# Recurrence keys transposed on VectorE instead of TensorE in a Hymba block

## The chip, the cores and the metric

The kernel runs on one core of a Trainium2 chip. The metric is the device time of one execution in microseconds (us); the median of three runs is compared. A profiled execution of the same program gives the trace from which the rows below are taken. Engines are named as in the profile: PE is TensorE's matmul, PEld its weight load, DVE VectorE, ACT ScalarE, POOL GpSimd, SP the engine whose queue issues the DMAs. L12 is line 12 of the kernel's file.

## The reference, cut to what matters

One layer: 512 tokens behind 16 learned meta tokens, width 2048. The input is normalised and projected by one matrix of 8320 columns. About half of these columns feed an RWKV-7 recurrence of 16 heads of 64 channels, the other half a short gated convolution. Both halves are gated, concatenated, projected back, added to the residual and normalised.

```python
def step(S, inp):
    r_t, w_t, k_t, v_t, kk_t, b_t = inp
    sa = jnp.einsum('bhvk,bhk->bhv', S, kk_t)
    S = (S * w_t[:, :, None, :]
         - sa[..., None] * b_t[:, :, None, :]
         + v_t[..., None] * k_t[:, :, None, :])
    y_t = jnp.einsum('bhvk,bhk->bhv', S, r_t)
    return S, y_t
...
hn = _rmsnorm(h_res, norm_in_g[l])
P = hn @ w_in[l]
...
y = _rwkv7_recurrence(rh, decay, kh, vh, kk, kk * ah)
...
mix = jnp.concatenate([y_a, y_b], axis=-1)
h_res = h_res + mix @ w_out[l]
```

The state S of a head is updated with two kinds of keys: b (taken off) and k (put on). These two kinds are what the change is about.

## The kernel before

**Projection.** The input is kept feature-major in SBUF (128 features on the partitions, 528 tokens along them), split into a high part `xh` and a low part `xl`. Each of the 65 tiles of 128 projection columns is made by `main()`, which runs `steps()` (L315): for each of 16 k-tiles and two ranges of tokens three matmuls, wh times xh, wh times xl and wl times xh. The tiles are called by what they hold: k, r, v and g for a pair of heads, C, h, B and gc for a group of the convolution, lora once. Their order is the list `plan`.

**Weights.** `prefetch()` loads 1024 columns (L134, tile `wr`, three buffers), which are two quarters of a projection tile. `split_w()` makes of each quarter (512 columns) the high part `wh`, a cast on ACT (L126), and the low part `wl`, a subtraction on DVE for even quarters and on POOL for odd ones (L127). There are six buffers each of wh and wl. Quarters are numbered in the order in which they are used, four to a projection tile.

**Order.** PE's order is written by hand. `mains()` is a generator of projection matmuls; `fill(ns)` and `until()` draw from it between the other matmuls, so that the projection covers what the recurrence's preparation waits for. The order on DVE, ACT, POOL and SP is made by a scheduler from the program and its priorities. `later(ns, fn)` puts DMAs to a due time on the clock of the drawn projection matmuls.

**Pairs.** Heads are handled in eight pairs, two times 64 channels on 128 partitions, time in nine chunks of 64 (the first holds the 16 meta tokens). `prepare(i)` makes for pair i the decay (`tz`, L521 and L522, plus one on POOL L581, a running sum `cc` on DVE L583), the operands `ar` (kk with decay, r with decay; L607) and `bk` (the keys: b, k and b again, so that either head finds its two kinds side by side: for head 0 b then k, for head 1 k then b), and the gram matmuls (L625) of chunk by chunk bk against ar, masked on DVE (L635) into `gt`. PE then transposes (L655) the two kinds of keys of chunks 0 to 7 from feature-major to token-major, 64 partitions by 128 columns to 128 partitions by 64, for each chunk and head; two PSUM tiles `zz` hold the result, and ACT copies them (L661) to `bt`. Norms (`n2`) and the bonus (`zb`, copied to r) follow. Between them, `gt` is sent through DRAM into 16x16 blocks, `d` and `nd`, and inverted on DVE (L701 to L734, the inverse chain). `invert()` widens the inverses of two pairs to 64x64.

**Operands in DRAM.** For each pair there is a buffer `opd`, 9 chunks of 128 rows of 576 floats. `stash()` (L567) stores into it: `spot(i, row, rows_n, c0, cn, step, o, n)` is n floats at offset o of rows_n rows from row on, over cn chunks. The offsets of a row are fixed; b is at O_B = 448 and k at O_K = 512, 64 floats each.

**Recurrence.** `recur()` walks over the chunks, loads the operands of each pair (tile `ct`, two buffers each, L870), and makes of the state `st`, the inverses and the values the products `rz` (L889), `z` (L906), the state's update `zs` (L941) and the outputs `zy` (L945). In `zs` the keys are the weights: 64 tokens on the partitions by 64 features, one matmul with u for b and one with v for k, for each head. Chunk 8 needs no update of the state.

**Output.** `split_mix()` brings the gated results back, and the output projection (L1070) runs over them at the end.

Of the kernel before, what the change touches and what calls it, by code (L numbers as in the profile page):

```python
# [9 lines left out]
F32 = mybir.dt.float32  # L10
# [8 lines left out]
P = 128  # L19
# [5 lines left out]
CH = 64  # L25
NCH = SEQ // CH + 1
# [12 lines left out]
O_AR, O_KK, O_BR, O_X, O_V, O_B, O_K = 0, 128, 256, 320, 384, 448, 512  # L39
# [37 lines left out]
def hymba_kernel(ctx: ExitStack, tc: tile.TileContext, xt, xtok, w_in, w_out, pv, lup, cst, msk, gf, out):  # L77
    nc = tc.nc
# [10 lines left out]
    ident = cs[:, C_ID : C_ID + P]  # L89
# [52 lines left out]
    cq = ph2.enter_context(tc.tile_pool(name="cq", bufs=1, side="right", reuse_waits="tile"))  # L142
# [12 lines left out]
    pz = ph1.enter_context(tc.tile_pool(name="pz", bufs=2, space=PSUM))  # L155
# [355 lines left out]
    def until(*key):  # L511
        while key not in ready:
            step()
# [41 lines left out]
    heads = [(h, slice(64 * h, 64 * h + 64), slice(64 - 64 * h, 128 - 64 * h)) for h in range(2)]  # L555
# [4 lines left out]
    def spot(i, row, rows_n, c0, cn, step, o, n):  # L560
        d = opd[i]
        return bass.AP(
            tensor=d.tensor, offset=d.offset + (c0 * P + row) * OPW + o, ap=[[OPW, rows_n], [step * P * OPW, cn], [1, n]]
        )

    def stash(i, src, o, n, row=0, rows_n=P, c0=0, cn=NCH, step=1):
        nc.sync.dma_start(spot(i, row, rows_n, c0, cn, step, o, n), src)  # L567

    def prepare(i):
        p = i % 2  # L570
        until("k", i)
        k = got["k", i]
        ar = cq.tile([P, NCH, 2, CH], F32, tag="ar", name=f"ar{i}")
        bk = cq.tile([P, NCH, 3, CH], F32, tag="bk", name=f"bk{i}")
# [4 lines left out]
        tz = low_rank(i, 0, up, hv[:, 0, i : i + 1], f"tz{i}", -1.0)  # L579
# [38 lines left out]
        fill(FW["gram_b" if p else "gram"])  # L618

        gt = cq.tile([P, 2, NCH, P], F32, tag=f"gt{p}", name=f"gt{i}")  # L620
        bt = cq.tile([P, 2, NCH - 1, CH], F32, tag="bt", name=f"bt{i}")

        def gram(z, c, c0):
            for h, hs, ho in heads:
                nc.tensor.matmul(  # L625
                    z[h][:, c - c0],
                    bk[hs, c, h : h + 2, :].rearrange("p a s -> p (a s)"),
                    ar[hs, c].rearrange("p a s -> p (a s)"),
                    start=True, stop=True,
                )  # L630

        def masked(z, c0, c1):
            with ahead():
                for h in range(2):
                    nc.vector.tensor_tensor(  # L635
                        out=gt[:, h, c0:c1],
                        in0=z[h],
                        in1=gmask[:, h].unsqueeze(1).to_broadcast([P, c1 - c0, P]),
                        op=ALU.mult,
                    )  # L640
# [7 lines left out]
        masked(zc, 4, 8)  # L648
        fill(FW["gram2"])
        ze = [pi.tile([P, 1, P], F32, tag=("misc", "ser")[h], name=f"g{i}_8_{h}") for h in range(2)]  # L650
        zz = [pz.tile([P, NCH - 1, CH], F32, tag="tz", name=f"bt{i}_{h}") for h in range(2)]
        gram(ze, 8, 8)
        for c in range(NCH - 1):
            for h, hs, ho in heads:
                nc.tensor.transpose(  # L655
                    zz[h][:, c], bk[hs, c, h : h + 2, :].rearrange("p a s -> p (a s)"),
                    ident[hs, 64 * h : 64 * h + 64],
                )
        masked(ze, 8, 9)
        for h in range(2):  # L660
            nc.scalar.copy(bt[:, h], zz[h])  # L661
        fill(FW["gram3"])
        n2 = tr(f"n2{i}")
        for j, (a, b) in enumerate(((0, 288), (288, LP))):
# [26 lines left out]
        d = cq.tile([NB, 256], F32, tag="d", name=f"d{i}").rearrange("p (s t) -> p s t", t=16)  # L691
# [22 lines left out]
        for m in (2, 4, 8):  # L714
            for b in range(16 // (2 * m)):
                o = b * 2 * m
# [33 lines left out]
        later(16500 if p else 33000, load_inverse)  # L750

        for h, hs, ho in heads:
            stash(i, bt[hs, h], O_B, CH, 64 * h, 64, 0, NCH - 1)
            stash(i, bt[ho, h], O_K, CH, 64 * h, 64, 0, NCH - 1)
        until("v", i)
        v = got["v", i]
        nc.vector.tensor_tensor(out=r, in0=r, in1=v[:, CH:LP], op=ALU.mult)
# [117 lines left out]
    def recur(ch):  # L875
        ops = {}
        load_chunk(ch, 0, range(NPAIR), ops)
        load_chunk(ch, 1, range(NPAIR), ops)
        st = None
        for c in range(NCH):  # L880
            last = c == NCH - 1
            z = [pz.tile([P, 2, 4, CH], F32, tag="tz", name=f"rz{c}_{e}") for e in range(2)]
            for k in range(4):
                for part in range(0 if c else 1, 2):
                    for e in range(2):
                        t = ops[c, 2 * k + e]
                        o = O_KK if part else O_AR
                        for h, hs, ho in heads:
                            nc.tensor.matmul(  # L889
                                z[e][ho if e else hs, 0, k], t[hs, o : o + CH],  # L890
                                t[hs, O_V : O_V + CH] if part else st[hs, 4 * e + k],
                                start=(part == 0 or c == 0), stop=(part == 1),
                            )
            pn = ch.tile([P, 2, 4, CH], F32, tag="pn", name=f"pn{c}", bufs=2)
            with ahead():
                for e in range(2):
                    nc.scalar.activation(pn[:, e], z[e][:, 0], AF.Copy, scale=-1.0)
            if c and not last:
                load_chunk(ch, c + 1, range(0, 4), ops)
            fill(FW["p"])  # L900
            for k in range(4):
                for e in range(2):
                    t = ops[c, 2 * k + e]
                    for h, hs, ho in heads:
                        m = ho if e else hs
                        nc.tensor.matmul(z[e][hs, 1, k], t[m, O_X : O_X + CH], pn[m, e, k], start=True, stop=True)  # L906
            u = ch.tile([P, 2, 4, CH], F32, tag="u", name=f"u{c}", bufs=2)
            with ahead():
                nc.scalar.copy(u[:, 0], z[0][:, 1])
                nc.vector.tensor_copy(u[:, 1], z[1][:, 1])  # L910
            if c and not last:
                load_chunk(ch, c + 1, range(4, NPAIR), ops)
            fill(FW["u"])
            here, there = [], []
            if not last:
                zs = pi.tile([P, NPAIR, CH], F32, tag="misc", name=f"zs{c}")
            if c:
                zy = pi.tile([P, NPAIR - 1, CH], F32, tag="ser", name=f"zy{c}")
            for k in range(4):
                for e in range(2):  # L920
                    t, j = ops[c, 2 * k + e], 4 * e + k
                    if not last:
                        here += [(zs, j, t, O_B, u[:, e, k], 0, 2), (zs, j, t, O_K, t[:, O_V : O_V + CH], 1, 2)]
                    if c and j < NPAIR - 1:
                        there += [
                            (zy, j, st[:, j], O_AR + CH, t, 0, 3),
                            (zy, j, t[:, O_V : O_V + CH], O_KK + CH, t, 1, 3),
                            (zy, j, u[:, e, k], O_BR, t, 2, 3),
                        ]
                    elif c:  # L930

                        here += [
                            (z[0][:, 0], 0, t, O_AR + CH, st[:, j], 0, 3),
                            (z[0][:, 0], 0, t, O_KK + CH, t[:, O_V : O_V + CH], 1, 3),
                            (z[0][:, 0], 0, t, O_BR, u[:, e, k], 2, 3),
                        ]
            for n in range(max(len(here), len(there))):
                if n < len(here):
                    d, j, t, o, x, a, b = here[n]
                    for h, hs, ho in heads:  # L940
                        nc.tensor.matmul(d[hs, j], t[hs, o : o + CH], x[hs], start=(a == 0), stop=(a == b - 1))  # L941
                if n < len(there):
                    d, j, x, o, t, a, b = there[n]
                    for h, hs, ho in heads:
                        nc.tensor.matmul(d[ho, j], t[hs, o : o + CH], x[hs], start=(a == 0), stop=(a == b - 1))  # L945
            if not last:
                new = ch.tile([P, NPAIR, CH], F32, tag="st", name=f"st{c}", bufs=2)
                scale = dd[:, c].unsqueeze(2).to_broadcast([P, NPAIR, CH])
                with ahead():
                    if c:  # L950
                        nc.vector.tensor_tensor(out=new, in0=zs, in1=st, op=ALU.add)
                    nc.vector.tensor_tensor(out=new, in0=new if c else zs, in1=scale, op=ALU.mult)
                st = new
            if c:
                norm(ch, (zy, z[0][:, 0, 0:1]), c)
            fill(FW["s"])
# [177 lines left out]
    for n in range(4):  # L1134
# [5 lines left out]
        for jj in range(first):  # L1140
# [3 lines left out]
            if n < 2 and jj % 4 == 2:  # L1144
                t, cols = jj // 4, slice(0, 512) if n == 0 else slice(512, DM)
# [89 lines left out]
```

## Time and profile before

| | us |
|---|---|
| runs | 1055.68, 1056.57, 1056.75; median 1056.57 |
| profiled execution, its own time | 1055.68 |
| its span in the profile | 1053.9 |
| its granted TensorE clock (share of full speed) | 0.996 |
| POOL, wl L127 | 150 times, 1.405 each |
| ACT, wh L126 | 312 times, 0.619 each |
| DVE, wl L127 | 162 times, 0.773 each |

Three kinds of rows appear below. A timeline row has the start in us, the busy time in us, engine, line and operation, output and inputs, partitions by elements, and how often it came in a row; brackets give the idle time of the engine before it and what ended it. A group row has line, engine, operation, shapes and count, then total busy time in us and the mean in ns of one, then the idle time just before such instructions. A waits row has the engine and its line, what it waited for, the total in us, the number of waits and the longest.

### The profile page before, as it was taken

To read this page: it belongs to the slowest core of one execution; us is meant where nothing else is said; L and a number is where in the kernel's file an instruction comes from. 1 tells how busy PE (TensorE), PEld (TensorE's weight loads), DVE (VectorE), ACT (ScalarE), POOL (GpSimd) and SP (SyncE) were. 2 spreads that over 40 slices of the span, in tenths; PEclk is the share of its full clock that TensorE was granted. 3 is DMA by queue.
4 is the path that set the end of the run, shared out by engine and by line. 5 is a ranking of instruction groups with operands and counts; after the bars stand their busy time and mean duration, and the time that the engine had idled before them with its cause. 6 is when DMAs were issued, how large, how long until landed. Compare 5 with 4: busy or idle time off the path is not lost.

```text
span 1053.9 us, 23986 instructions
## 1 busy us (share of the span) xinstructions
PE 1035.8 (98%) x9973; PEld 945.8 (90%) x9973; DVE 565.4 (54%) x1072; ACT 366.3 (35%) x682; POOL 307.8 (29%) x315
## 2 busy tenths in 40 slices
PE   7999999999999999999999999999999999999996
PEld 6999998999998999989999989888898988888885
DVE  6774965559563658653757642455454771212132
ACT  7553422433332433233443232222222432323232
POOL 0132413324222323132323231323233242424232
PEclk9999999999999999999999999999999999999999
DMA  8446475364843363753364648777644978323314
GB/s 295 137 121 158 117 177 142 108 154 119 207 141 114 109 161 116 175 155 114 104 170 129 169 134 288 233 216 247 184 144 110 280 225 305 98 85 98 100 61 160
DMA packets 182893, 167.49 MB, mean 159 GB/s; under 512 B 120960, under 2 KB 143232, under 8 KB 182400
## 3 DMA queue, kind: packets, MB, share of 16 engines
q1 hardware_dynamic: 182208, 164.90, 54.0%
q8 instruction: 78, 1.28, 0.5%
q10 hardware_dynamic: 576, 1.07, 0.3%
q14 instruction: 31, 0.25, 0.1%
HBM read 129.05 MB, written 36.88 MB: 157 GB/s over the span
## 4 chain that ended last, share of the span: by engine, by line
PE 91%; DVE 4%; issue 2%; DMA 1%; ACT 1%; POOL 1%; SPq 0%; DVEq 0%; ACTq 0%; POOLq 0%
PE o L1070 17%; PE ps_g L315 9%; PE ps_C L315 9%; PE ps_gc L315 9%; PE ps_k L315 9%; PE ps_B L315 8%; PE ps_h L315 8%; PE ps_r L315 7%; PE ps_v L315 7%; PE g L625 2%; PE zs L941 1%; PE rz L889 1%; PE ps_lora L315 1%; PE zy L945 1%; DMA wq<-in_w_in_dram 1%
## 5 line engine op out<-in xcount | busy, mean ns | idle before, releaser
L127 POOL TENSOR_TENSOR wl<-wr,wh 128x512 fp32r<-128x512 f32 x150 | 210.4, 1405 | 458.0 <-ACT wh L126 428.0
L126 ACT CAST wh<-wr 128x512 fp32r<-128x512 f32 x312 | 188.8, 619 | 390.0 <-PE o L1070 93.6
L127 DVE TENSOR_TENSOR wl<-wr,wh 128x512 fp32r<-128x512 f32 x162 | 124.4, 773 | 244.0 <-ACT wh L126 243.6
L1070 PE MATMUL o<-wh,m 128*128 128x512 f32 (+1 forms) x484 | 145.3, 384 | 0.0
L1070 PEld LDWEIGHTS o<-wh,m 128*128 128x128 f32 x484 | 89.6, 188 | 21.3
L1070 PE MATMUL o<-wl,m 128*128 128x512 f32 (+1 forms) x242 | 92.6, 389 | 0.0
L315 PE MATMUL ps_k<-xl,wh 128*128 128x264 f32 x256 | 73.1, 286 | 0.0
L315 PE MATMUL ps_v<-xh,wh 128*128 128x264 f32 x256 | 73.1, 286 | 0.0
L315 PE MATMUL ps_g<-xh,wl 128*128 128x258 f32 (+1 forms) x256 | 72.2, 282 | 0.9 <-DVE wl L127 0.8
L315 PE MATMUL ps_r<-xh,wh 128*128 128x258 f32 (+1 forms) x256 | 72.2, 282 | 0.8 <-ACT wh L225 0.8
L315 PE MATMUL ps_k<-xh,wh 128*128 128x264 f32 x256 | 73.0, 285 | 0.0
L315 PE MATMUL ps_h<-xh,wl 128*128 128x258 f32 (+1 forms) x256 | 72.8, 284 | 0.0
L315 PE MATMUL ps_k<-xh,wl 128*128 128x264 f32 x256 | 72.7, 284 | 0.0
L315 PE MATMUL ps_v<-xh,wl 128*128 128x264 f32 x256 | 72.7, 284 | 0.0
L315 PE MATMUL ps_v<-xl,wh 128*128 128x264 f32 x256 | 72.7, 284 | 0.0
L315 PE MATMUL ps_g<-xl,wh 128*128 128x258 f32 (+1 forms) x256 | 72.5, 283 | 0.0
L315 PE MATMUL ps_h<-xh,wh 128*128 128x258 f32 (+1 forms) x256 | 72.3, 282 | 0.0
L315 PE MATMUL ps_C<-xh,wh 128*128 128x258 f32 (+1 forms) x256 | 72.3, 282 | 0.0
L315 PE MATMUL ps_g<-xh,wh 128*128 128x258 f32 (+1 forms) x256 | 72.3, 282 | 0.0
L315 PE MATMUL ps_C<-xh,wl 128*128 128x258 f32 (+1 forms) x256 | 72.3, 282 | 0.0
L315 PE MATMUL ps_h<-xl,wh 128*128 128x258 f32 (+1 forms) x256 | 72.2, 282 | 0.0
L315 PE MATMUL ps_r<-xl,wh 128*128 128x258 f32 (+1 forms) x256 | 72.1, 282 | 0.0
(271 smaller groups left out, 2706.3 us busy)
## 6 DMA issues: line engine op xcount, KB each, us to landing
wr<-in_w_in_dram SPq DMA_DIRECT2D x127, 512.0 KB
ct<-opd SPq DMA_DIRECT2D x64, 288.0 KB
wr<-in_w_out_dram SPq DMA_DIRECT2D x32, 512.0 KB
opd<-ar SPq DMA_DIRECT2D x8, 576.0 KB
opd<-gt SPq DMA_DIRECT2D x16, 288.0 KB
opd<-bt SPq DMA_DIRECT2D x32, 128.0 KB
xres<-in_xtok_dram SPq DMA_DIRECT2D x4, 768.0 KB
out_dram<-xres SPq DMA_DIRECT2D x6, 512.0 KB
```

What stands on the lines that cost most here:

```text
L126: nc.scalar.copy(hi, rq)
L127: eng.tensor_tensor(out=lo, in0=rq, in1=hi.bitcast(F32), op=ALU.subtract)
L315: nc.tensor.matmul(ps[r], ww[:, w], xx[:, kt, a:b], start=(kt == 0 and n == 0), stop=(kt == KT - 1 and n == 2))
L625: nc.tensor.matmul(z[h][:, c - c0], bk[hs, c, h : h + 2, :].rearrange("p a s -> p (a s)"), ar[hs, c].rearrange("p a s -> p (a s)"), start= ...
L889: nc.tensor.matmul(z[e][ho if e else hs, 0, k], t[hs, o : o + CH], t[hs, O_V : O_V + CH] if part else st[hs, 4 * e + k], start=(part == 0 ...
L941: nc.tensor.matmul(d[hs, j], t[hs, o : o + CH], x[hs], start=(a == 0), stop=(a == b - 1))
L945: nc.tensor.matmul(d[ho, j], t[hs, o : o + CH], x[hs], start=(a == 0), stop=(a == b - 1))
L1070: nc.tensor.matmul(ps[t + p], mm[:, tk], ww[:, o], start=(jj == 0 and q == 0), stop=(jj == KT - 1 and q == 2))
```

## The change

`bt` is made by two DVE transposes per pair, ahead of the gram matmuls. Each transposes every 32x32 block of the 128 partitions in place: for chunks 0 to 7, it takes one of the two kinds of keys as it lies in `bk` (slot 0 and slot 1) and writes it with a step of two floats, so that the two slots alternate in `bt`. A 32x32 transpose brings each block of 32 tokens and 32 features to the right way round but leaves the blocks where they were; the addresses of the stores put them at their places: eight stores per pair, one for each block of 32 features (b), head (h) and block of 32 tokens (t), instead of four. The 16 PE transposes, the two PSUM tiles and the two ACT copies per pair are gone.

In DRAM the row of a token now has, from offset O_B on, 128 floats in which b and k alternate. `recur()` reads each kind with a step of two floats as the weights of `zs`. The order of PE's instructions is otherwise the same; the order on the other engines is made anew by the scheduler.

```diff
@@ -618,7 +618,11 @@
         fill(FW["gram_b" if p else "gram"])
 
         gt = cq.tile([P, 2, NCH, P], F32, tag=f"gt{p}", name=f"gt{i}")
-        bt = cq.tile([P, 2, NCH - 1, CH], F32, tag="bt", name=f"bt{i}")
+
+
+        bt = cq.tile([P, NCH - 1, 2, CH // 2, 2], F32, tag="bt", name=f"bt{i}")
+        for a in range(2):
+            nc.vector.transpose(bt[:, :, :, :, a], bk[:, 0 : NCH - 1, a].rearrange("p c (t s) -> p c t s", t=2))
 
         def gram(z, c, c0):
             for h, hs, ho in heads:
@@ -648,17 +652,8 @@
         masked(zc, 4, 8)
         fill(FW["gram2"])
         ze = [pi.tile([P, 1, P], F32, tag=("misc", "ser")[h], name=f"g{i}_8_{h}") for h in range(2)]
-        zz = [pz.tile([P, NCH - 1, CH], F32, tag="tz", name=f"bt{i}_{h}") for h in range(2)]
         gram(ze, 8, 8)
-        for c in range(NCH - 1):
-            for h, hs, ho in heads:
-                nc.tensor.transpose(
-                    zz[h][:, c], bk[hs, c, h : h + 2, :].rearrange("p a s -> p (a s)"),
-                    ident[hs, 64 * h : 64 * h + 64],
-                )
         masked(ze, 8, 9)
-        for h in range(2):
-            nc.scalar.copy(bt[:, h], zz[h])
         fill(FW["gram3"])
         n2 = tr(f"n2{i}")
         for j, (a, b) in enumerate(((0, 288), (288, LP))):
@@ -750,8 +745,12 @@
         later(16500 if p else 33000, load_inverse)
 
         for h, hs, ho in heads:
-            stash(i, bt[hs, h], O_B, CH, 64 * h, 64, 0, NCH - 1)
-            stash(i, bt[ho, h], O_K, CH, 64 * h, 64, 0, NCH - 1)
+            for b in range(2):
+                for t in range(2):
+                    stash(
+                        i, bt[64 * h + 32 * b : 64 * h + 32 * b + 32, :, t].rearrange("p c s a -> p c (s a)"),
+                        O_B + 64 * b, 64, 64 * h + 32 * t, 32, 0, NCH - 1,
+                    )
         until("v", i)
         v = got["v", i]
         nc.vector.tensor_tensor(out=r, in0=r, in1=v[:, CH:LP], op=ALU.mult)
@@ -920,7 +919,8 @@
                 for e in range(2):
                     t, j = ops[c, 2 * k + e], 4 * e + k
                     if not last:
-                        here += [(zs, j, t, O_B, u[:, e, k], 0, 2), (zs, j, t, O_K, t[:, O_V : O_V + CH], 1, 2)]
+                        bb = t[:, O_B : O_B + 2 * CH].rearrange("p (s a) -> p a s", a=2)
+                        here += [(zs, j, bb[:, 0], 0, u[:, e, k], 0, 2), (zs, j, bb[:, 1], 0, t[:, O_V : O_V + CH], 1, 2)]
                     if c and j < NPAIR - 1:
                         there += [
                             (zy, j, st[:, j], O_AR + CH, t, 0, 3),
@@ -938,7 +938,8 @@
                 if n < len(here):
                     d, j, t, o, x, a, b = here[n]
                     for h, hs, ho in heads:
-                        nc.tensor.matmul(d[hs, j], t[hs, o : o + CH], x[hs], start=(a == 0), stop=(a == b - 1))
+                        w = t[hs, o : o + CH] if o else t[hs]
+                        nc.tensor.matmul(d[hs, j], w, x[hs], start=(a == 0), stop=(a == b - 1))
                 if n < len(there):
                     d, j, x, o, t, a, b = there[n]
                     for h, hs, ho in heads:
```

## The prediction

> **What bounds the kernel now.** I read the page's busy line and chain first, then a table of three stretches, then TensorE's list of waits.
>
> ```profile
> PE 1035.8 (98%) x9973; PEld 945.8 (90%) x9973; DVE 565.4 (54%) x1072; ACT 366.3 (35%) x682; POOL 307.8 (29%) x315
> PE 91%; DVE 4%; issue 2%; DMA 1%; ACT 1%; POOL 1%; SPq 0%; DVEq 0%; ACTq 0%; POOLq 0%
> ```
> ```profile
> 26.00:1040.00 1014.00, 1009.29 (x9823) 923.89 (x9823) 542.63 (x1021) 343.45 (x638) 301.41 (x293) 1.00 0.54 154
> ```
> ```profile
> PE rz L941 <- issue: 1.6, 1, 1.6
> ...
> PE zy L945 <- issue: 1.3, 1, 1.3
> ...
> PE ps_B L315 <- DVE wl L127: 0.9, 1, 0.9
> ...
> PE ps_g L315 <- DVE wl L127: 0.8, 2, 0.4
> ```
>
> The third line reads: stretch, busy time of PE, PEld, DVE, ACT and POOL, granted clock, DMA share, GB/s. From 26 to 1040 us PE is idle for 4.7 us of 1014, at full clock. The kernel is one uninterrupted stream of matmuls. An edit therefore counts in two ways only: matmuls that leave the stream, and waits of PE that go or come. In the two "issue" waits, both in the recurrence, PE waited for nothing that the profile shows; I let them stand. The feeding waits, 0.9 + 0.8 us, are on wl (L127), the low halves of the weights: a quarter of a tile is cast on ACT (L126), subtracted on DVE or POOL, and then multiplied.
>
> **The change part by part: TensorE's transposes.** Sixteen a pair leave the stream. What they take is the distance from the gram matmul ahead of them to the projection matmul behind them, less what that gram would take alone.
>
> ```profile
> 82.79 0.49 PE L625 MATMUL g<-ar,bk 64*128 64x128 f32 x4
> 83.11 0.66 PE L655 MATMUL bt<-cs,bk 64*128 64x64 f32 x16
> 83.70 0.38 PE L315 MATMUL ps_r<-xl,wh 128*128 128x258 f32 x1
> ...
> 213.24 2.06 PE L625 MATMUL g<-ar,bk 64*128 64x128 f32 x32
> 215.22 0.39 PE L315 MATMUL ps_v<-xh,wh 128*128 128x264 f32 x1
> ```
>
> From 82.79 to 83.70 is 0.91 us. Thirty-two gram rows take 215.22 - 213.24 = 1.98, so four take 0.25. The transposes are worth 0.66 a pair, and 8 x 0.66 = **-5.3 us**, which nothing can hide, since PE has no slack.
>
> **The copies and the new transposes.**
>
> ```profile
> L661 ACT COPY bt<-bt 128x512 f32<-128x512 f32 x16 | 8.9, 585 | 15.1 <-PE bt L655 15.1
> ...
> L785 DVE STREAM_TRANSPOSE xn<-xT 128x512 f32<-128x512 f32 x8 | 5.6, 703 | 0.0
> L719 DVE TENSOR_TENSOR prod<-d,y 72x512 f32<-72x512 f32 x8 | 8.4, 1056 | 0.1
> L728 DVE TENSOR_TENSOR prod<-y,tt 72x512 f32<-72x512 f32 x8 | 9.3, 1157 | 0.1
> ```
>
> ACT loses 16 x 0.585 = 9 us. DVE gains 16 block transposes of 128x512: 703 ns each by the same operation on a dense tile, 1157 by a strided 512-wide row, so 11 to 18 us. Neither engine sets the end (54% and 35% busy): directly both cost 0, and the cover is the projection stream. If a transpose stood ahead of a quarter's subtraction with no slack, it would cost PE its 0.7 to 1.2. So the places where PE is fed just in time decide. I went through those in the two programs' instruction orders, since on every engine but PE and the DMA queue the order is the scheduler's.
>
> **Waits that go.** At 159.63 PE waits 0.91 because a conv tile's chain (eviction hh, L334; product u; cv; subtraction) ends late.
>
> ```profile
> 154.26 1.29 POOL L401 TENSOR_TENSOR u<-u,hh 128x514 f32<-128x514 f32 x1 [11.02 <-DVE hh L334]
> ```
>
> In the changed order the hh evictions stand two 512-wide operations of the 16x16 inverse chain earlier, about 1.9 us, so u starts earlier and the 0.9 goes. The next two waits, 0.39 us at 256.84 and its twin in the next two pairs, come from casts queued on ACT behind rk_h:
>
> ```profile
> 249.35 0.73 ACT L351 ACTIVATE sh_r<-pr_r,pvt 128x512 f32<-128x512 f32 x1 [2.01 <-DVE pr_r L334]
> ...
> 253.88 0.62 ACT L551 CAST rk_h<-r 128x512 fp32r<-128x512 f32 x1 [3.80 <-DVE r L610]
> 254.41 3.22 ACT L126 CAST wh<-wr 128x512 fp32r<-128x512 f32 x6
> ```
> ```profile
> 256.10 1.28 DVE L127 TENSOR_TENSOR wl<-wr,wh 128x512 fp32r<-128x512 f32 x2
> ```
> ```profile
> 256.84 0.39 PE L315 MATMUL ps_g<-xh,wl 128*128 128x258 f32 x1 [0.39 <-DVE wl L127]
> ...
> 267.18 0.71 PE L625 MATMUL g<-ar,bk 64*128 64x128 f32 x3
> 268.43 0.39 PE L315 MATMUL ps_g<-xh,wh 128*128 128x256 f32 x1
> ```
>
> In the changed order these casts no longer stand behind rk_h: -0.8. The last gram waits for its bank's mask: 268.43 - 267.18 = 1.25 against the 0.91 above, 0.34 lost; the masks come some 2 us earlier in two odd pairs: twice 0.34 to 0.4, -0.8. Together **-2.5 us**.
>
> **Waits that come: odd pairs.** In pairs 3, 5 and 7 the scheduler moves the cast of one quarter behind sh_r and its subtraction behind ar (L607). In pair 3 that quarter is the 74th, and PE first reads it at 250.22.
>
> ```profile
> 236.51 0.16 DVE L701 TENSOR_SCALAR nd<-nd 72x16 f32<-72x16 f32 x1
> 240.85 1.34 DVE L583 TENSOR_TENSOR_SCAN cc<-smask,tz 128x576 f32<-128x576 f32 x1
> 251.85 0.69 DVE L607 TENSOR_TENSOR ar<-r,e 128x512 f32<-128x512 f32 x1
> ```
> ```profile
> 237.04 1.66 POOL L581 TENSOR_SCALAR tz<-tz 128x576 f32<-128x576 f32 x1 [2.74 <-ACT tz L528]
> ```
> ```profile
> 250.22 0.28 PE L315 MATMUL ps_v<-xh,wh 128*128 128x264 f32 x1
> ```
>
> With the old times ar ends at 252.54, the subtraction at 253.15, and PE, which wants the low half at 250.22 + 0.24 = 250.46, waits 2.7. But the same move takes that subtraction from ahead of nd: the inverse chain starts about 1.6 us earlier (234.9), and the scan cc, freed, waits only for POOL's tz, done at 238.70 instead of 240.85. Everything that hangs on cc is 2 us earlier: ar at 249.85, subtraction done near 251.1, a wait of 0.7. Pairs 5 and 7 have one more subtraction (L545) moved out of the way: half, 0.35 each. I take 0.7 + 2 x 0.35 = 1.4, between 0 and 3 x 2.7 = 8.1.
>
> **The h tile behind an odd pair.** Its first quarter's subtraction moves behind the whole inverse chain, and nd behind the second eviction pr_g:
>
> ```profile
> 283.31 0.16 DVE L701 TENSOR_SCALAR nd<-nd 72x16 f32<-72x16 f32 x1
> 284.32 0.43 DVE L334 TENSOR_TENSOR pr_g<-ps_g,rs 128x256 f32<-128x256 f32 x1 [0.23 <-PE ps_g L315]
> 294.02 0.68 DVE L734 TENSOR_REDUCE y<-prod 72x64 f32<-72x512 f32 x1
> ```
> ```profile
> 295.77 0.28 PE L315 MATMUL ps_h<-xh,wl 128*128 128x258 f32 x1
> ```
>
> The chain ended at 294.70; started 0.7 later it ends at about 295.4, the subtraction at 296.05, and PE wants it at 295.77: 0.3, three times, 0.9. At pair 2, ar stands behind a block transpose and a subtraction:
>
> ```profile
> 211.62 0.69 DVE L607 TENSOR_TENSOR ar<-r,e 128x512 f32<-128x512 f32 x1
> ```
>
> It ends at 212.31 now; 0.70 + 0.61 later is 213.6, against the gram at 213.24: 0.3. The other even pairs have 2 us to spare. Sum of the new waits: **+2.6**, between 0 and 9.3.
>
> **Strided weights.** The recurrence's L941 now reads its weights for both kinds of key at every second float.
>
> ```profile
> L941 PEld LDWEIGHTS zs<-ct 64*64 64x64 f32 x256 | 12.8, 135 | 0.0
> ...
> L625 PEld LDWEIGHTS g<-ar,bk 64*128 64x128 f32 x288 | 17.9, 187 | 2.4 <-DVE gt L635 0.2
> ```
>
> Sixty-four more columns cost 187 - 135 = 52 ns. If stride slowed a load as it slowed DVE above (1157/703 = 1.65), a load would cost 34 ns more, and 256 loads 8.7 us if none overlapped. Below it is 0: nothing suggests a gain. No row of before has a strided weight load; the DVE rows stride by 8 and 16 floats, and two is nearest to dense, so I take **0**, and keep 8.7 for the range.
>
> [...]
>
> **The DMA queue.** Four stores of a pair become eight of half the size.
>
> ```profile
> 232.12 2.64 SPq L567 DMA_DIRECT2D opd<-bt  x4
> 235.48 3.62 SPq L567 DMA_DIRECT2D opd<-vs  x7
> 239.21 1.47 SPq L134 DMA_DIRECT2D wr<-in_w_in_dram  x3
> ```
>
> Four more issues are 2.6 us of SP's queue. Behind them stand the value stores and the weight loads of 239.21, which feed quarters read by PE 10 us later: cost 0, cover the three weight buffers; without it the 2.6 would reach PE. Runs stay 256 bytes, so the volume is the same.
>
> **Sum.** -5.3 - 2.5 + 2.6 = -5.2. The profiled run took 1055.68, 1.8 of them outside its span of 1053.9; its span would be 1048.7, its run 1050.5. That run is the lowest of the three; on their median of 1056.57 the forecast is **1051.4**.
>
> **The rivals.** *Strided weight loads decide* (slower). Place: the zs bursts of eight chunks; price 34 ns x 256 = +8.7; it decides as soon as a strided load is longer than the matmul it should hide behind by more than 5.2/256 = 20 ns. For: PEld is 90% busy. Against: the step is small. 1051.4 + 8.7 = 1060.1.
>
> *The odd pairs stall in full*: cc does not come earlier, because POOL's tz or ACT ahead of it is late too. Then 8.1 stands where 1.4 stood: 1058.1. For: the order does put the subtraction behind ar. Against: tz's end at 238.70.
>
> *The scheduler's waits go and none come*: -5.3 - 2.5 = 1048.8. For: the new waits are small differences. Against: three separate places.
>
> *Nothing is gained*: the weights' path, not PE, sets the pace, and PE waits for what it saved: 1056. Against: ACT's casts were waiting, DMA is at 0.54, and PE lacks 4.7 us of 1014.
>
> **How the numbers follow.** Forecast 0.60 (its own range 1049.8 to 1053.5), strided loads 0.12, odd pairs 0.13, no new waits 0.10, nothing gained 0.05. The measurement tells 0.2% from no change, that is 1054.5 and 1058.7. Faster: 0.60 + 0.10 and 0.03 from a milder case of the odd pairs, 0.73; the same: the other 0.10 of the odd pairs and 0.05 of nothing gained, 0.15; slower: the strided loads, 0.12. From 1048.7 to 1058.2 holds every case but the strided loads, and leaves a little for sizes beyond the bounds.
>
> **What would show it.** PE's busy time 5 us lower, and the stretch between the last gram and the next projection matmul 0.25 instead of 0.91; no wait of ps_B on wl near 159; waits of ps_v of 0.3 to 0.7 behind wl in odd pairs, and of ps_h of 0.3; DVE transposes of 0.70 us; a weight load of zs of 135 ns. Loads of 160 ns or more, ps_v waits near 2.7, or wr landing after ACT is free would prove me wrong.

## The result, and the profile after

The changed kernel took 1061.63 us in the median of four runs (1059.99 to 1063.40), the kernel before 1056.12 in the same comparison: a ratio of 1.0051, with an interval of 1.0034 to 1.0068. It is slower by half a per cent. The forecast was 1051.4, in a range of 1048.7 to 1058.2.

The profiled execution took 1059.99 us, with a span of 1058.2, which is 4.3 above the span before. From its page come the busy line and the shares of the chain that ended last:

```profile
PE 1034.8 (98%) x9845; PEld 943.4 (89%) x9845; DVE 572.1 (54%) x1088; ACT 358.4 (34%) x666; POOL 316.6 (30%) x315
PE 82%; DVE 6%; issue 3%; POOL 3%; SPq 2%; DMA 2%; ACT 1%; DVEq 0%; POOLq 0%; ACTq 0%
```

PE runs 128 matmuls fewer, as it should, but its busy time fell by 1.0 us only, and the chain runs through PE for 82% of the span where it was 91. Where it left PE stands in the list of PE's waits (total, number, longest):

```profile
PE ps_v L315 <- POOL wl L127: 4.2, 2, 2.1
PE ps_h L315 <- DVE wl L127: 2.6, 3, 0.9
...
PE ps_v L315 <- DVE wl L127: 1.5, 3, 0.7
...
PE rz L942 <- issue: 1.2, 1, 1.2
PE ps_B L315 <- DVE wl L127: 0.8, 1, 0.8
PE zy L946 <- issue: 0.7, 1, 0.7
```

The waits of ps_g are gone, that of ps_B was to go and is there (0.91 before, 0.8 now), and three groups are new, 8.3 us together. The largest of them was in no term of the prediction: ps_v waits for a subtraction on POOL. The timeline of POOL, DVE and PE around the first of the two waits (pair 5):

```profile
402.55 5.63 POOL L127 TENSOR_TENSOR wl<-wr,wh 128x512 fp32r<-128x512 f32 x1
```
```profile
402.20 0.68 DVE L127 TENSOR_TENSOR wl<-wr,wh 128x512 fp32r<-128x512 f32 x1
402.81 0.67 DVE L720 TENSOR_REDUCE tt<-prod 72x64 f32<-72x512 f32 x1
403.40 0.73 DVE L610 SCALAR_TENSOR_TENSOR r<-r,hv,ta 128x512 f32<-128x512 f32 x1
404.06 0.68 DVE L127 TENSOR_TENSOR wl<-wr,wh 128x512 fp32r<-128x512 f32 x1
404.66 1.18 DVE L723 TENSOR_TENSOR prod<-y,tt 72x512 f32<-72x512 f32 x1
405.76 0.68 DVE L552 TENSOR_TENSOR rk_l<-r,rk_h 128x512 fp32r<-128x512 f32 x1
406.37 0.68 DVE L127 TENSOR_TENSOR wl<-wr,wh 128x512 fp32r<-128x512 f32 x1
406.97 0.68 DVE L729 TENSOR_REDUCE y<-prod 72x64 f32<-72x512 f32 x1
407.56 1.29 DVE L625 STREAM_TRANSPOSE bt<-bk 128x512 f32<-128x512 f32 x2
```
```profile
402.94 0.39 PE L315 MATMUL ps_v<-xh,wl 128*128 128x264 f32 x1 [0.36 <-DVE wl L127]
...
408.23 0.39 PE L315 MATMUL ps_v<-xh,wl 128*128 128x264 f32 x1 [2.12 <-POOL wl L127]
```

One subtraction lies on POOL for 5.63 us, from 402.55 to 408.18, and PE goes on at 408.23. Alone it takes 1.27, as two in a row do in 2.54 us in a row of 284.86 below. In between DVE runs six operations with two tensor inputs, with no gap and at their usual lengths (0.68 to 1.18 us; in the kernel before, the means of the same four kinds were 685 to 1157 ns). POOL ends 1.2 us after the last of them gives way to a reduction and the transposes, each of which reads one tensor. So the quarter was cast in time: 1.27 us from 402.55 would have ended 2.3 us before PE stopped at 406.11. In pair 7 the same row takes 7.26 us, from 556.03 on. In the kernel before, the same quarter of pair 5 was done ten microseconds earlier, at its usual length:

```profile
392.20 1.28 POOL L127 TENSOR_TENSOR wl<-wr,wh 128x512 fp32r<-128x512 f32 x1 [0.33 <-ACT wh L126]
```

The rest of the trace points at DVE too. Of POOL's 150 subtractions, 70 overlap with no DVE operation that reads two tensors from SBUF, and none of these takes more than 1.31 us; all 31 that take over 1.4 us overlap with some. Overlap alone doesn't decide, as 40 others that have over 0.3 us of it stay under 1.4.

In pair 7 the same wait has a second cost. The windows around it (busy time of PE, PEld, DVE, ACT and POOL, granted clock, DMA share, GB/s):

```profile
562.00:563.30 1.30, 0.00 (x0) 0.00 (x0) 1.30 (x4) 0.00 (x0) 1.30 (x2) 1.00 0.00 0
563.30:566.70 3.40, 3.35 (x15) 3.35 (x16) 1.10 (x3) 0.00 (x0) 2.47 (x2) 0.52 0.56 180
566.70:570.00 3.30, 3.30 (x29) 3.30 (x28) 1.53 (x4) 1.99 (x3) 1.29 (x1) 0.98 0.71 190
```

For 3.4 us after the wait the granted clock is 0.52, and 15 matmuls pass where 29 do afterwards. That counts as busy time of PE, which is one reason why its total fell so little. Behind the equal wait of pair 5 the clock stayed at 1.00:

```profile
408.20:411.60 3.40, 3.37 (x27) 3.37 (x28) 1.09 (x3) 0.00 (x0) 2.47 (x2) 1.00 0.55 178
```

### The profile page after: what moved, and what is told of

It reads as the page before. It is cut to its first block, busy times and chain, and to the rows that moved or that the text cites. A ratio compares the mean times of both kernels' runs of the same rounds, so it can differ in the third digit from the quotient of the medians.

```text
span 1058.2 us, 23748 instructions
## 1 busy us (share of the span) xinstructions
PE 1034.8 (98%) x9845; PEld 943.4 (89%) x9845; DVE 572.1 (54%) x1088; ACT 358.4 (34%) x666; POOL 316.6 (30%) x315
## 3 DMA queue, kind: packets, MB, share of 16 engines
q8 instruction: 77, 1.26, 0.5%
## 4 chain that ended last, share of the span: by engine, by line
PE 82%; DVE 6%; issue 3%; POOL 3%; SPq 2%; DMA 2%; ACT 1%; DVEq 0%; POOLq 0%; ACTq 0%
PE o L1071 17%; PE ps_gc L315 9%; PE ps_k L315 9%; PE ps_B L315 8%; PE ps_h L315 8%; PE ps_r L315 8%; PE ps_v L315 7%; PE ps_C L315 5%; PE ps_g L315 4%; POOL wl L127 2%; PE g L629 2%; SPq L567 1%; PE zs L942 1%; DMA wq<-in_w_in_dram 1%; DVE prod L714 1%
## 5 line engine op out<-in xcount | busy, mean ns | idle before, releaser
L127 POOL TENSOR_TENSOR wl<-wr,wh 128x512 fp32r<-128x512 f32 x150 | 217.7, 1454 | 470.3 <-ACT wh L126 443.4
L315 PE MATMUL ps_r<-xh,wl 128*128 128x258 f32 (+1 forms) x256 | 72.1, 282 | 0.0
```

The costliest lines, as they stand in the source:

```text
L127: eng.tensor_tensor(out=lo, in0=rq, in1=hi.bitcast(F32), op=ALU.subtract)
L315: nc.tensor.matmul(ps[r], ww[:, w], xx[:, kt, a:b], start=(kt == 0 and n == 0), stop=(kt == KT - 1 and n == 2))
```

## The experiments

The cases to tell apart: A, the quarters of weights are fed late because the schedule around the stores changed; B, the strided weight loads; C, the DVE transposes.

**Stores of 64 rows.** The changed kernel with four stores of keys instead of eight.

```diff
-for b in range(2):
-    for t in range(2):
-        stash(i, bt[64*h+32*b : 64*h+32*b+32, :, t]..., O_B + 64*b, 64, 64*h + 32*t, 32, 0, NCH-1)
+for t in range(2):
+    stash(i, bt[hs, :, t]..., O_B + 64*t, 64, 64*h, 64, 0, NCH-1)
...
-nc.gpsimd.tensor_copy(dd[:, :, place[i]], e1[:, :, CH])
+nc.gpsimd.tensor_scalar(out=dd[:, :, place[i]], in0=e1[:, :, CH], scalar1=1e-25, ...)
```

> The changed kernel, but with four stores of keys per pair, each of 64 partitions, in place of eight of 32 (same bytes, same 256-byte runs). The keys land in wrong rows, and the decay between chunks is scaled to almost nothing so that the numbers stay finite: the output is not the reference's. In this program's order the casts of the first two v quarters of odd pairs stand ahead of sh_r again, and the first h quarter's subtraction ahead of the inverse chain. Theory A (the eight 32-row stores make the scheduler place these casts and subtractions late, and PE waits for them): the three kinds of waits go (ps_v 5.7 us, ps_h 2.6) and the time falls to 1050 to 1053. Theory B (strided weight loads cost the 9 us): they are still strided, so 1060 to 1063. Theory C (the DVE transposes load DVE and block POOL): they are still there, so 1058 to 1063.

Measured: 1054.62 us, ratio 0.9997 (0.9982 to 1.0013). All waits of ps_v and ps_h are gone, with the DVE transposes and the strided reads still there, so neither B nor C carries the loss. The time is above A's 1053, and new waits came. The first in its list of PE's waits is:

```profile
PE ta L521 <- ACT tz L526: 2.5, 3, 0.8
```

Two casts now stand ahead of the activation of tz, and the next matmul waits for its bank.

**Transposes put back.** The changed kernel, with L655 and L661 of before running beside it.

```diff
 gram(ze, 8, 8)
+for c in range(NCH - 1):
+    for h, hs, ho in heads:
+        nc.tensor.transpose(zz[h][:, c], ...)
 masked(ze, 8, 9)
+for h in range(2):
+    nc.scalar.copy(unread[h], zz[h])
```

> The changed kernel with the sixteen TensorE transposes, their two PSUM tiles and the two ACT copies of each pair put back; the copies go to a tile that nobody reads, so the result is still right. The orders of the casts are those of the changed kernel. Measures what the transposes are worth to PE: by the step from trace to trace (0.49 us a pair) it is 3.9 us slower than the changed kernel, 1065 to 1066; by the prediction's 0.66 a pair 5.3 slower, 1067; by a theory that PE does not set the pace, no slower, 1061 to 1062.

Measured: 1061.24 us, ratio 1.0043 (1.0029 to 1.0057), which the interval doesn't tell from the changed kernel's 1.0051: the expected 3.9 us did not show. In its trace the transposes take 0.5 us in seven of the eight pairs, and the waits behind them shrink:

```profile
PE ps_v L315 <- POOL wl L127: 2.9, 2, 1.4
```

They were 4.2. While PE waits at such places for something that does not move with it, what PE saves ahead of the place is waited off there. The traces bear this out in part only: against 3.5 us for the transposes, the waits behind them (those of ps_v on POOL, of ps_h and of ps_B) are some 2.7 us shorter, and the profiled execution of this run, its slowest, still has a span 2.9 us longer than the changed kernel's.

**Strided reads alone.** The kernel before, with both kinds of keys read with a step of two.

```diff
-here += [(zs, j, t, O_B, u[:, e, k], 0, 2), (zs, j, t, O_K, ...)]
+bb = t[:, O_B : O_B + 2 * CH].rearrange("p (s a) -> p a s", a=2)
+here += [(zs, j, bb[:, 0], 0, u[:, e, k], 0, 2), (zs, j, bb[:, 1], 0, ...)]
```

> The kernel before, in which only the recurrence reads its two kinds of keys with a step of two floats. They read the wrong floats, and the decay between chunks is scaled to almost nothing to keep the numbers finite: the output is not the reference's. All orders are those of before. Theory A: the loads stay at 135 ns and the time within 0.2% of before, 1055 to 1058. Theory B: loads of 160 ns or more and 1060 to 1065.

Measured: 1056.08 us, ratio 1.0001 (0.9992 to 1.0011). The loads in the changed kernel's own groups of instructions (busy, mean ns of one):

```profile
L942 PEld LDWEIGHTS zs<-ct 64*64 64x64 f32 x256 | 13.1, 136 | 0.0
```

They took 135 ns before. B is out.

**Stores of 32 rows alone.** The kernel before, each of its stores of keys cut in two.

```diff
-stash(i, bt[hs, h], O_B, CH, 64 * h, 64, 0, NCH - 1)
+for b in range(2):
+    stash(i, bt[64*h+32*b : 64*h+32*b+32, h], O_B, CH, 64*h + 32*b, 32, 0, NCH - 1)
```

(The stores to O_K likewise.)

> The kernel before with each of its four stores of keys per pair cut into two of 32 partitions; everything else as before, the result right. In this order the first h quarter's subtraction stands behind the inverse chain, as in the changed kernel, while the v quarters' casts stay where they were. Theory A: waits of ps_h on wl come in three pairs, 0.2 to 0.9 each (PE is not ahead of its old times here), in all 1057 to 1059. Theories B and C: 1055 to 1057, no change.

Measured: 1076.19 us, ratio 1.0185 (1.0169 to 1.0201). The waits of ps_h came, 1.7 us, but most of the loss is at a place that nobody named. In this order six casts stand behind sh_v, and PE needs them before:

```profile
PE ps_g L315 <- DVE wl L127: 7.2, 4, 1.9
PE ps_g L315 <- ACT wh L126: 5.9, 3, 2.0
PE ps_h L315 <- DVE wl L127: 1.7, 3, 0.7
```
```profile
258.97 0.73 ACT L341 ACTIVATE sh_v<-pr_v,pvt 128x528 f32<-128x528 f32 x1 [2.44 <-DVE pr_v L334]
259.61 3.20 ACT L126 CAST wh<-wr 128x512 fp32r<-128x512 f32 x6
```
```profile
262.50:265.90 3.40, 3.21 (x15) 3.21 (x16) 3.40 (x3) 0.31 (x1) 2.96 (x2) 0.50 0.57 159
```

The last row is a window behind one of these waits: the clock is at half again, here for 6.8 us from 261.9 on. Three such stretches, 17 us in all, stand in this trace, and PE is busy for 1044.4 us where it was 1035.8. So 32-row stores upset the schedule in either kernel, by different places. Why the scheduler answers so to a store's rows was not tried.

**The late quarters on DVE.** The changed kernel, with two of its 312 subtractions moved from POOL to DVE.

```diff
-nc.gpsimd if q and j > 8 else nc.vector
+nc.gpsimd if q and j > 8 and j not in (61, 85) else nc.vector
```

> The changed kernel, with the two odd quarters whose subtraction on POOL ended 2.1 us late (the second v quarter of pairs 5 and 7) subtracted on DVE instead. Theory A1 (POOL's subtraction is as late as its cast and no more; it is queued too late): DVE is no earlier, ps_v still waits 1.5 to 2.5 us in both pairs. Theory A2 (the cast is in time, and DVE's operations with two inputs block POOL's, so that 1.3 us became 5.6): on DVE it takes 0.7 us in its turn, and the ps_v waits at that quarter fall below 0.7 each; 1057 to 1060 in all, as the low clock behind one of the waits goes too.

Measured: 1055.10 us, ratio 0.9995 (0.9985 to 1.0005), some 6 us below the changed kernel and under the 1057 to 1060 expected, though DVE has two operations more. Both waits on POOL are gone, and the low clock at 563 with them (this trace has one at 731 instead, in the recurrence):

```profile
PE ps_h L315 <- DVE wl L127: 2.5, 3, 1.0
PE rz L942 <- issue: 1.7, 1, 1.7
...
PE ps_v L315 <- DVE wl L127: 1.5, 3, 0.7
```

That is A2: the casts were in time, and POOL was held.

**Stores put off.** The changed kernel, its stores of keys due 20 or 8 us later; then 20 us with more projection between the low-rank matmuls.

```diff
+def put_keys():
     for h, hs, ho in heads:
...
+later(20000, put_keys)
```

> The changed kernel with its eight stores of keys of each pair put off by 20 us of drawn projection matmuls; the result is right. The casts of the odd pairs stand as in the run with 64-row stores. Theory A: as that run, 1053 to 1056, with waits of ta on tz (0.8 in three pairs) in place of ps_v and ps_h. Rival (the stores slow the weights themselves, by the bytes on the queues): they still move the same bytes in the same pieces, so 1059 to 1063.

Measured: 1060.64 us, ratio 1.0043 (1.0028 to 1.0059): a miss. The waits of ps_v and ps_h are gone, but a mask is 1.8 us late in the first odd pair, and the last pair's stores push the recurrence's first loads back. Half the clock is granted at both places, for 3.4 us from 132.6 and for 6.8 us from 654.9, and PE's busy time is 1039.1 us where it is 1032.2 in the next run, with equally many matmuls:

```profile
PE rz L891 <- DMA ct<-opd: 2.5, 7, 0.4
PE ta L521 <- ACT tz L526: 2.5, 3, 0.8
PE g L629 <- DVE gt L639: 1.8, 1, 1.8
```

> As the run before, but put off by 8 us. The first two v quarters stand early as there, and sh_v now ahead of four later casts. Theory A: 1052 to 1056, with ta on tz 0.8 in three pairs; if the stores at 8 us meet the weights' loads, waits of ps_g on wl or wh of 1 us a pair and 1056 to 1060.

Measured: 1055.55 us, ratio 0.9998 (0.9986 to 1.0010), with ta on tz 2.5 and one wait of ps_g of 1.5: within what was expected, and no gain.

```diff
-    ... lora=2200 ...
+    ... lora=2800 ...
```

> As the run with 20 us, and the projection drawn between the low-rank matmuls is 2.8 us in place of 2.2, to cover the wait of ta on tz. If that wait is only the cover's shortage, three times 0.8 go and the time is 1051 to 1053; if what follows in the pair (grams, inverse chain) is later by 1 to 2 us and PE waits for it, 1053 to 1058.

Measured: 1064.84 us, ratio 1.0089 (1.0072 to 1.0106). The wait of ta went, and others took its place: ps_h 5.4 us, the grams' masks 3.5, 2.1 on xn. This was above either expectation.

**Three places mended.** The changed kernel, with the work moved to the engine that is free at each place.

```diff
-nc.gpsimd if q and j > 8 else nc.vector
+nc.gpsimd if (q and j > 8 and j not in (61, 85)) or j in (44, 68, 92) else nc.vector
...
-nc.gpsimd.tensor_tensor(out=u[:, 0:n], ...)
+(nc.gpsimd if i else nc.vector).tensor_tensor(out=u[:, 0:n], ...)
```

> The changed kernel with five quarters and one product on another engine: the two odd v quarters on DVE as in the run that did this alone, the first h quarter of pairs 3, 5 and 7 on POOL instead of DVE (there it does not stand behind the inverse chain), and the product u of the first conv group on DVE instead of POOL. The result is right. Theory A (PE's saved time comes out once these waits are gone): 1055.1 less 2.5 for ps_h less 0.8 for ps_B, 1051 to 1053, with only ps_v's three waits of 0.4 to 0.7 left. Rival (other work is late next at the same places): 1054 to 1056.

Measured: 1051.33 us, ratio 0.9956 (0.9944 to 0.9968): faster than both kernels. What these moves would give the kernel before was not run; the next run, which has PE's transposes, is below 1 too, so not all of the gain is due to the transposes. Its waits, and POOL doing both quarters where the changed kernel's DVE did one of them at 294.21, behind its inverse chain:

```profile
PE ps_v L315 <- DVE wl L127: 1.5, 3, 0.7
...
PE ps_B L315 <- DVE wl L127: 0.2, 1, 0.2
```
```profile
284.86 2.54 POOL L127 TENSOR_TENSOR wl<-wr,wh 128x512 fp32r<-128x512 f32 x2 [5.85 <-ACT wh L126]
```

> The run with three places mended, and the sixteen TensorE transposes, their PSUM tiles and the two ACT copies of each pair put back as before (their result unread). Measures what the transposes are worth where no wait takes their place: 3.0 to 3.9 us above that run by the step in the traces (0.49 a pair), 5.3 by the prediction's 0.66, nothing if waits still take it.

The edit is that of the second experiment. Measured: 1054.05 us, ratio 0.9984 (0.9975 to 0.9992), 2.7 above the run without them. From trace to trace the transposes step by 0.49 to 0.51 us in seven of the eight pairs, 3.5 in all, within the 3.0 to 3.9 expected; the medians' 2.7 is just below. In pair 1 they are free, since the last gram there waits for its mask in either case.

**DVE transposes alone.** The kernel before, with the two transposes added; ACT writes over what they write.

```diff
 bt = cq.tile([P, 2, NCH - 1, CH], F32, tag="bt", name=f"bt{i}")
+for a in range(2):
+    nc.vector.transpose(bt[:, a], bk[:, 0 : NCH - 1, a])
```

> The kernel before with two DVE transposes per pair added at the place where the changed kernel has them; they write into bt, which is then written over by ACT as before, so the result is right. All else is as before. Theory C (the DVE transposes' own time and their hold on POOL cost it): 3 to 6 us slower. Theory A (they are hidden, apart from a place or two): within 1 us of before.

Measured: 1057.23 us, ratio 1.0014 (1.0004 to 1.0024), 1.5 more than before: between A and C.

```profile
PE ps_g L315 <- DVE wl L127: 3.5, 3, 1.8
```

ps_g waited 0.8 before. Where a subtraction had no slack, the transposes ahead of it are paid, as the prediction's condition said with its 0.7 to 1.2; the sum took nothing for it. In pairs 3 and 5 this cost 0.5 each. In pair 7 both transposes stand ahead of the subtraction, which itself took 1.26 us instead of 0.68 beside one of POOL's, 1.7 in all. In the changed kernel this price did not come up, since its waits of ps_g are gone.

## Why the prediction was wrong

Sizes from here on are steps: by how much the difference in start of one and the same projection matmul, between the two traces, changes from the last one ahead of a place to the first one behind it.

| Term | predicted | measured |
|---|---|---|
| start, ahead of the first transposes | 0 | -0.4 |
| PE transposes | -5.3 | -3.4 |
| ps_B wait at 159 | -0.9 | -0.1 |
| ps_g waits on wl | -0.8 | -1.4 |
| mask of the last gram | -0.8 | -0.8 |
| ps_v on DVE's quarter, three pairs | +1.4 | +1.9 |
| ps_v on POOL's quarter, two pairs | none | +4.5 |
| low clock behind one of these | none | +1.6 |
| ps_h, three pairs | +0.9 | +3.1 |
| pair 2's gram | +0.3 | 0 |
| strided loads | 0 | 0 |
| recurrence's "issue" waits | 0 | -0.7 |

The measured column sums to +4.3, as much as the span grew; the prediction's sum was -5.2. Left out are some 0.1 us that the second matmul behind each wait adds, 0.4 in all, and small steps elsewhere that take this back.

**The step that failed** is "Waits that come: odd pairs". It followed one quarter, the DVE one, and that part held: "0.7 + 2 x 0.35" against waits of 0.73, 0.36 and 0.37. But the same move of the casts behind sh_r took the next quarter along, whose subtraction is POOL's. I had not followed it, and had no price for two engines that hold each other up. The list of before had shown it, had I read one row more, on POOL:

```profile
561.82 3.84 POOL L127 TENSOR_TENSOR wl<-wr,wh 128x512 fp32r<-128x512 f32 x1 [8.82 <-ACT wh L126]
```

The run with the two quarters on DVE shows that this cause, with the low clock behind it, is worth some 6 us: without it the kernel is as fast as before (0.9995), not yet faster. The rest of the forecast gain went to ps_h, ps_B and the price of the transposes, below; with the first two mended as well the ratio was 0.9956.

The rival in which the odd pairs stall in full named the right place, but its condition did not come: ar of pair 3 ended at 249.26, earlier even than the 249.85 of the forecast.

That DVE holds POOL up rests on the overlaps above (none of the 70 subtractions without one is over 1.31 us, and all 31 over 1.4 have one) and on the run with the two quarters on DVE. POOL, under way at 402.55, did not end after the reduction of 402.81, with a two-input operation queued behind it, but after that of 406.97, with a transpose behind it. No run here shows why.

**ps_B stayed for the same reason.** The forecast moved u earlier with its evictions, and u did start at 152.41 instead of 154.26, but beside a two-input operation on DVE:

```profile
152.41 2.15 POOL L401 TENSOR_TENSOR u<-u,hh 128x514 f32<-128x514 f32 x1 [10.01 <-DVE hh L334]
```
```profile
152.25 1.15 DVE L723 TENSOR_TENSOR prod<-y,tt 72x512 f32<-72x512 f32 x1
```

It took 2.15 where it had taken 1.29, and half of the lead was lost; PE, itself 0.9 earlier by then, took the rest. With u on DVE the wait fell to 0.2, and with the transposes put back, where u took 1.30 on POOL, the list has no wait of ps_B. The size is not steady from trace to trace: the run with strided reads alone, in the order of before, has 0.3 here where before had 0.9.

**ps_h was mis-sized.** The place and the mechanism were right (a subtraction behind the inverse chain), 0.3 a pair became 0.9.

```profile
294.21 0.68 DVE L127 TENSOR_TENSOR wl<-wr,wh 128x512 fp32r<-128x512 f32 x1
```
```profile
294.94 0.39 PE L315 MATMUL ps_h<-xh,wl 128*128 128x258 f32 x1 [0.93 <-DVE wl L127]
```

The subtraction ended at 294.89, earlier than the 296.05 forecast. But I held it against 295.77, when PE wanted it before; PE, 1.9 us ahead by then, wanted it at 293.9. A date for PE must move with what PE is to gain.

**The transposes were over-priced.** I took the 0.91 us of gram and transposes less 0.25 for a gram of four rows. In the changed kernel that gram takes 0.42 on its own:

```profile
82.40 0.49 PE L629 MATMUL g<-ar,bk 64*128 64x128 f32 x4
82.82 0.39 PE L315 MATMUL ps_r<-xl,wh 128*128 128x258 f32 x1
```

So 0.49 a pair leave, not 0.66: the cadence of a long burst is no price for a short one. In pair 1 nothing leaves: PE is 0.88 ahead, and the gram has to wait for the masks.

```profile
125.24 2.47 DVE L639 TENSOR_TENSOR gt<-g,cs 128x512 f32<-128x512 f32 x4
```
```profile
128.18 0.39 PE L315 MATMUL ps_C<-xh,wh 128*128 128x258 f32 x1
```

The masks end at 127.71, and the matmul behind the gram starts at 128.18, 0.84 ahead of the 129.02 of before.

**Right:** the ps_g waits and the masks; the DVE transposes' own length (703 ns forecast, 696 measured); the strided loads at nothing. A load read with a step of two floats took 136 ns where it took 135 dense, and the run with strided reads alone came to 1.0001. The rival that named the slower side was the strided loads, so the time came near that rival's 1060.1 for another cause.

## What to carry to other kernels

When a change moves work between queues, follow every instruction that moves with it, on each engine, and ask of each pair that now overlaps whether one can hold up the other; a row on POOL that is several times its usual length (here 5.63 and 7.26 us for 1.27) is the sign. Compare each arrival with the consumer's new time, not with its old one. A saving on the bounding engine shows only if no fixed wait stands behind it: by the medians, the same sixteen transposes a pair were worth nothing that could be measured in one schedule and 2.7 us in another.

## What the runs showed of the hardware that was not expected

DVE and POOL held each other up both ways here. In the run with the late quarters on DVE it was DVE that waited, its row of 1.18 grown to 2.24 beside POOL's:

```profile
405.35 2.24 DVE L723 TENSOR_TENSOR prod<-y,tt 72x512 f32<-72x512 f32 x1
```

A wait of about 2 us on PE cost 1.6 more in pair 7, by a granted clock of 0.50 to 0.52 for 3.4 us. Here 2.11 us of waiting were enough in pair 7, and 2.12 were not in pair 5, where the clock stayed at 1.00. Which of the two it will be was not settled. Length alone does not tell. In the run with stores put off by 20 us the clock went to half at 654.9 behind four waits of at most 0.45 us; in the run with strided reads alone it did at 730.6, behind a wait of 1.76, while the kernel before has a wait of 1.63 at the same place, in the same order, and no low clock. One execution of each kernel was traced, so it is not known how often the changed kernel pays the 1.6.

A wait cost more here than its row says. The one at 408.23 has 2.12 us in its row, but the matmul behind it stepped by 2.28, and the next matmul came 0.23 us after it (408.46) where the stream has 0.12. So some 0.3 us are to be added to that one.
